# A sum of absolute differences: the kernel's instructions put into the first block, with semaphores of their own

**Chip, cores, metric.** One core of one Trainium2 chip. The metric is the device time of the kernel in microseconds (us). "The span" is what the profiler recorded of one execution; it is some 1.8 us shorter than the time.

## The reference

```python
batch, dim = 1024, 4096          # x, y: float32 [1024, 4096]
def reference(x, y, axis):       # axis = -1
    return np.sum(np.abs(x - y), axis=axis).astype(np.float32)
```

33.55 MB have to be read from memory; 4 KB are written.

## The kernel before

128 partitions hold 8 rows each (K = 8, H = 4). Rows 0 to 3 of x and y are loaded by two large transfers, rows 4 to 6 of x by a third; the y rows 4 to 6 go, one by one, into the y buffers that the first subtractions set free. The last row comes in four pieces. VectorE subtracts, ScalarE takes the absolute value and sums along the row. A semaphore is a counter that a finished transfer or operation raises and on which an instruction can wait (VectorE's first recorded wait starts 0.03 us after the landing at 41.49 us that it waits for). A block is a stretch of the built program that ends in a branch: the first block holds the opening barrier, the final one each engine's drain instructions and the closing barriers, in which GpSimd waits until all engines have drained (its wait is recorded at 83.89 us, 0.03 us behind the last of these drains, SyncE's at 83.86). A recording layer puts in the semaphores and waits (`tc`); only the first two loads and the first two waits of VectorE were placed by hand into the first block (`at_entry`).

```python
PIECES = [1984, 1088, 640, 384]; ROW6 = [2048, 1024, 1024]
at_entry(nc, lambda: nc.sync.dma_start(out=xa, in_=xr[:, 0:H, :]).then_inc(early[0], 16), "Drain")
at_entry(nc, lambda: nc.scalar.dma_start(out=yb, in_=yr[:, 0:H, :]).then_inc(early[1], 16), "Drain")
nc.sync.dma_start(out=xb[:, 0:H - 1, :], in_=xr[:, H:K - 1, :])
...
for sem in early:
    at_entry(nc, lambda: nc.vector.wait_ge(sem, 16), "UnconditionalBranch")
for k in range(H):
    whole(xa[:, k, :], yb[:, k, :], k)                    # tensor_sub, then activation with accum_out
    if k < H - 1:
        nc.sync.dma_start(out=yb[:, k, :], in_=yr[:, H + k, :])
        continue
    for w in PIECES: ...                                  # x piece and y piece, in turn
...                                                       # rows 4, 5; row 6 in three parts
for i, w in enumerate(PIECES):
    if i == 1:
        nc.vector.reduce_sum(out=ro[:, K - 2:K - 1], in_=part6, axis=AX)
    if i < n_part:
        nc.vector.tensor_sub(...); nc.scalar.activation(..., accum_out=last[:, i:i + 1])
    else:
        nc.vector.tensor_sub(out=last[:, n_part:n_part + w], ...)
        nc.vector.reduce_sum(out=ro[:, K - 1:K], in_=last, axis=AX, apply_absolute_value=True)
nc.sync.dma_start(out=orr, in_=ro)
```

Of the kernel before, what the change touches and what calls it, by code (L numbers as in the profile page):

```python
# [5 lines left out]

F32 = mybir.dt.float32
ABS = mybir.ActivationFunctionType.Abs
AX = mybir.AxisListType.X

PIECES = [1984, 1088, 640, 384]
ROW6 = [2048, 1024, 1024]


def at_entry(nc, emit, before):

    hook = nc.inst_callbacks[-1]
    lower = nc._always_lower_symbolic_ap
    nc.remove_inst_callback(hook)
    nc._always_lower_symbolic_ap = False  # L20
    try:
        ins = emit().ins
    finally:
        nc._always_lower_symbolic_ap = lower
        nc.push_inst_callback(hook)
    here = nc.cur_bb.bb.instructions
    main = nc.main_func.blocks[0].instructions
    at = [i for i, x in enumerate(here) if x.name == ins.name]
    assert len(at) == 1
    mine = here.pop(at[0])  # L30
    first = next(i for i, x in enumerate(main) if x.engine == mine.engine and x.opcode == before)
    main.insert(first, mine)


@with_exitstack
def kernel(ctx, tc, x, y, axis, out):
    nc = tc.nc
    P = nc.NUM_PARTITIONS
    R, C = x.shape
    K = R // P  # L40
    xr = x.rearrange("(p k) c -> p k c", p=P, k=K)
    yr = y.rearrange("(p k) c -> p k c", p=P, k=K)
    orr = out.rearrange("(p k) -> p k", p=P, k=K)
    assert sum(PIECES) == C
    n_part = len(PIECES) - 1
    n6 = len(ROW6)
    H = K // 2
    ps = ctx.enter_context(tc.tile_pool(name="ps", bufs=1))
    with tc.manual_schedule():
        xa = nc.alloc_sbuf_tensor("xa_rows", [P, H, C], F32).ap()  # L50
        xb = ps.tile([P, H, C], F32, tag="xb")

        yb = nc.alloc_sbuf_tensor("yb_rows", [P, H, C], F32).ap()
        ro = ps.tile([P, K], F32, tag="ro")
        part6 = ps.tile([P, n6], F32, tag="part6")

        last = ps.tile([P, n_part + PIECES[-1]], F32, tag="last")
        early = [tc.alloc_semaphore("early_x"), tc.alloc_semaphore("early_y")]
        at_entry(nc, lambda: nc.sync.dma_start(out=xa, in_=xr[:, 0:H, :]).then_inc(early[0], 16), "Drain")
        at_entry(nc, lambda: nc.scalar.dma_start(out=yb, in_=yr[:, 0:H, :]).then_inc(early[1], 16), "Drain")  # L60
        nc.sync.dma_start(out=xb[:, 0:H - 1, :], in_=xr[:, H:K - 1, :])

        def whole(tx, ty, k):
            nc.vector.tensor_sub(out=tx, in0=tx, in1=ty)  # L64
            nc.scalar.activation(tx, tx, ABS, accum_out=ro[:, k:k + 1])  # L65

        for sem in early:
            at_entry(nc, lambda: nc.vector.wait_ge(sem, 16), "UnconditionalBranch")  # L68
        for k in range(H):
            whole(xa[:, k, :], yb[:, k, :], k)  # L70
            if k < H - 1:
                nc.sync.dma_start(out=yb[:, k, :], in_=yr[:, H + k, :])
                continue
            o = 0
            for w in PIECES:
                nc.sync.dma_start(out=xb[:, k, o:o + w], in_=xr[:, K - 1, o:o + w])
                nc.sync.dma_start(out=yb[:, k, o:o + w], in_=yr[:, K - 1, o:o + w])
                o += w
        for k in range(H - 2):
            whole(xb[:, k, :], yb[:, k, :], H + k)  # L80
        o = 0
        for i, w in enumerate(ROW6):
            tx, ty = xb[:, H - 2, o:o + w], yb[:, H - 2, o:o + w]
            nc.vector.tensor_sub(out=tx, in0=tx, in1=ty)  # L84
            nc.scalar.activation(tx, tx, ABS, accum_out=part6[:, i:i + 1])  # L85
            o += w
        tx, ty = xb[:, H - 1, :], yb[:, H - 1, :]
        o = 0
        for i, w in enumerate(PIECES):
            s = slice(o, o + w)  # L90
            if i == 1:
                nc.vector.reduce_sum(out=ro[:, K - 2:K - 1], in_=part6, axis=AX)  # L92
            if i < n_part:
                nc.vector.tensor_sub(out=tx[:, s], in0=tx[:, s], in1=ty[:, s])  # L94
                nc.scalar.activation(tx[:, s], tx[:, s], ABS, accum_out=last[:, i:i + 1])  # L95
            else:
                nc.vector.tensor_sub(out=last[:, n_part:n_part + w], in0=tx[:, s], in1=ty[:, s])  # L97
                nc.vector.reduce_sum(out=ro[:, K - 1:K], in_=last, axis=AX, apply_absolute_value=True)  # L98
            o += w
        nc.sync.dma_start(out=orr, in_=ro)  # L100


# [1 line left out]
_INS = ['x', 'y', 'axis']  # L104
_OUTS = [((1024,), 'float32')]

_NUMBERS = {'axis': -1}


# [26 lines left out]
```

## Time and profile before

| | before |
|---|---|
| median time | 86.28 us (86.19 to 86.42, 3 runs) |
| span of the profiled run | 84.5 us |
| rows 0 to 3 of x and y landed, VectorE starts | 41.49, 41.80 us |
| last load landed | 80.68 us |
| final reduction starts | 81.53 us |
| store issued, landed | 82.11, 83.53 us |

How to read it: the loads run without a break to 80.7 us (DMA share 0.99 to 1.01 in every stage up to 78 us), and what follows the last landing is a tail of fixed steps. A gain must come from that tail, or from VectorE or ScalarE where the tail waits for them. The lines of the chain and of the last microseconds stand in the prediction. This is the view of the end line L131, one row per engine and operation: count, shortest, median and longest duration in ns, first and last start in us. SP is SyncE; q marks its sequencer.

```profile
L131 SPq EVENT_SEMAPHORE  x6: 17/28/28, 83.5 to 84.5; - x6
L131 SPq DRAIN  x3: 7/7/7, 83.8 to 84.1; - x3
L131 DVEq COMPARE_BRANCH  x1: 47/47/47, 41.6 to 41.6; - x1
```

Four of the six SyncE waits (28 ns each) stand between the store's landing at 83.5 and the first drain at 83.8; the other two belong to the final barriers. The one recorded branch is VectorE's, which carries a wait.

### The profile page before, as it was taken

The page shows a single profiled execution, that of the slowest core. Times are in us where ns is not written, and L with a number is a line of the kernel's source. Part 1 is how long each engine was busy: PE and PEld are TensorE (multiplying, and loading weights), DVE is VectorE, ACT ScalarE, POOL GpSimd, SP SyncE. Part 2 cuts the span into 40 slices and gives each one's busy share as a digit, 9 for nine tenths or more (in the row PEclk, how much of TensorE's full clock was granted, in tenths as well). Part 3 has the DMA queues.
Part 4 walks back from the last instruction along what each step waited for, and adds up shares of the span by engine and source line. Part 5 has one row for each costly group of instructions (what it writes and reads, how often), then busy time and mean ns, then how long its engine had stood idle before and what let it go on. Part 6 is the DMA issues. An engine that isn't in the chain of part 4 may idle for free.

```text
span 84.5 us, 110 instructions
## 1 busy us (share of the span) xinstructions
DVE 36.5 (43%) x15; ACT 31.2 (37%) x25; POOL 0.2 (0%) x4
## 2 busy tenths in 40 slices
DVE  0000000000000000000299999999298997988860
ACT  5000000000000000000001979797971968999950
POOL 0000000000000000000000000000000000000000
DMA  9479999995799999957999888999999999999700
GB/s 496 186 310 496 496 496 496 496 465 217 310 496 496 496 496 496 465 217 310 512 581 395 372 372 372 411 450 411 457 403 450 419 394 421 421 407 402 290 0 2
DMA packets 2160, 33.56 MB, mean 397 GB/s; under 512 B 368, under 2 KB 624, under 8 KB 1392
## 3 DMA queue, kind: packets, MB, share of 16 engines
q1 hardware_dynamic: 2016, 25.17, 70.8%
q10 hardware_dynamic: 144, 8.39, 22.9%
HBM read 33.55 MB, written 0.00 MB: 397 GB/s over the span
## 4 chain that ended last, share of the span: by engine, by line
DMA 67%; DVE 16%; ACT 13%; issue 1%; ACTq 0%; DVEq 0%
DMA yb_rows<-in_y_dram 67%; DVE xa_rows L64 10%; DVE xb L64 5%; ACT xb L85 5%; ACT xb L65 4%; ACT xb L95 4%; DVE ro L98 1%; ACTq L131 0%; DVEq L131 0%; DVEq L68 0%
## 5 line engine op out<-in xcount | busy, mean ns | idle before, releaser
L64 DVE TENSOR_TENSOR xa_rows<-xa_rows,yb_rows 128x4096 f32<-128x4096 f32 x4 | 17.4, 4420 | 41.8 <-DMA yb_rows<-in_y_dram 41.8
L65 ACT ACTIVATE xa_rows<-xa_rows 128x4096 f32<-128x4096 f32 x4 | 14.5, 3617 | 45.9 <-DVE xa_rows L64 45.9
L64 DVE TENSOR_TENSOR xb<-xb,yb_rows 128x4096 f32<-128x4096 f32 x2 | 8.9, 4426 | 2.0 <-DMA yb_rows<-in_y_dram 2.0
L65 ACT ACTIVATE xb<-xb 128x4096 f32<-128x4096 f32 x2 | 7.2, 3617 | 3.4 <-DVE xb L64 3.4
L84 DVE TENSOR_TENSOR xb<-xb,yb_rows 128x1024 f32<-128x1024 f32 (+1 forms) x3 | 4.6, 1576 | 0.5 <-DMA yb_rows<-in_y_dram 0.5
L94 DVE TENSOR_TENSOR xb<-xb,yb_rows 128x1984 f32<-128x1984 f32 (+2 forms) x3 | 4.3, 1447 | 0.9 <-DMA yb_rows<-in_y_dram 0.9
L85 ACT ACTIVATE xb<-xb 128x1024 f32<-128x1024 f32 (+1 forms) x3 | 4.0, 1323 | 0.0
L95 ACT ACTIVATE xb<-xb 128x1984 f32<-128x1984 f32 (+2 forms) x3 | 3.7, 1229 | 0.0
L65 ACT ACT_TABLE_LOAD x1 | 1.3, 1283 | 0.9 <-PEq L117 0.9
L65 ACT ACTIVATION_READ_ACCUMULATOR xa_rows<-xa_rows 128x1 f32 x4 | 0.7, 186 | 0.0
L98 DVE TENSOR_REDUCE ro<-last 128x1 f32<-128x387 f32 x1 | 0.6, 556 | 0.2 <-ACT xb L95 0.2
L97 DVE TENSOR_TENSOR last<-xb,yb_rows 128x384 f32<-128x384 f32 x1 | 0.6, 558 | 0.1
L95 ACT ACTIVATION_READ_ACCUMULATOR xb<-xb 128x1 f32 x3 | 0.6, 187 | 0.0
L85 ACT ACTIVATION_READ_ACCUMULATOR xb<-xb 128x1 f32 x3 | 0.6, 185 | 0.0
L65 ACT ACTIVATION_READ_ACCUMULATOR xb<-xb 128x1 f32 x2 | 0.4, 186 | 0.0
L92 DVE TENSOR_REDUCE ro<-part 128x1 f32<-128x3 f32 x1 | 0.2, 156 | 0.2 <-ACT xb L85 0.2
L117 POOL MEMSET const-bfloat16-1.0<- 128x1 bf16 x1 | 0.1, 101 | 0.0
L117 POOL MEMSET const-uint8-127<- 128x1 uint8 x1 | 0.1, 101 | 0.0
L117 POOL MEMSET const-float32-0.0<- 128x1 f32 x1 | 0.1, 98 | 0.2 <-issue 0.2
L117 POOL MEMSET const-float32-1.0<- 128x1 f32 x1 | 0.1, 98 | 0.0
## 6 DMA issues: line engine op xcount, KB each, us to landing
xb<-in_x_dram SPq DMA_DIRECT2D x1, 6144.0 KB, 54.9
yb_rows<-in_y_dram SPq DMA_DIRECT2D x3, 2048.0 KB, 15.0
xb<-in_x_dram SPq DMA_DIRECT2D x1, 992.0 KB, 17.6
yb_rows<-in_y_dram SPq DMA_DIRECT2D x1, 992.0 KB, 16.1
xb<-in_x_dram SPq DMA_DIRECT2D x1, 544.0 KB, 17.1
yb_rows<-in_y_dram SPq DMA_DIRECT2D x1, 544.0 KB, 17.9
xb<-in_x_dram SPq DMA_DIRECT2D x1, 320.0 KB, 18.3
yb_rows<-in_y_dram SPq DMA_DIRECT2D x1, 320.0 KB, 18.6
```

Of the source, the lines that this page charges most:

```text
L64: nc.vector.tensor_sub(out=tx, in0=tx, in1=ty)
L65: nc.scalar.activation(tx, tx, ABS, accum_out=ro[:, k:k + 1])
L84: nc.vector.tensor_sub(out=tx, in0=tx, in1=ty)
L85: nc.scalar.activation(tx, tx, ABS, accum_out=part6[:, i:i + 1])
L92: nc.vector.reduce_sum(out=ro[:, K - 2:K - 1], in_=part6, axis=AX)
L94: nc.vector.tensor_sub(out=tx[:, s], in0=tx[:, s], in1=ty[:, s])
L95: nc.scalar.activation(tx[:, s], tx[:, s], ABS, accum_out=last[:, i:i + 1])
L97: nc.vector.tensor_sub(out=last[:, n_part:n_part + w], in0=tx[:, s], in1=ty[:, s])
L98: nc.vector.reduce_sum(out=ro[:, K - 1:K], in_=last, axis=AX, apply_absolute_value=True)
L117: nc = _bacc.Bacc("TRN2", target_bir_lowering=False, num_devices=1)
```

## The change

The intent: put all of the kernel's instructions into the first block and give them their own semaphores, so that each piece needs one wait (x and y count on the same semaphore up to 32), no load waits for a reused semaphore, and one wait stands behind the store instead of one per semaphore. Transfers, operations, sizes and their order are the same.

```diff
-        for sem in early:
-            at_entry(nc, lambda: nc.vector.wait_ge(sem, 16), "UnconditionalBranch")
+    put(lambda: nc.sync.dma_start(out=xa, in_=xr[:, 0:H, :]).then_inc(s_first, 16), early=True)
+    put(lambda: nc.scalar.dma_start(out=yb, in_=yr[:, 0:H, :]).then_inc(s_first, 16), early=True)
+    put(lambda: nc.sync.dma_start(out=xb[:, 0:H - 1, :], in_=xr[:, H:K - 1, :]).then_inc(s_xb, 16))
...
+        put(lambda: nc.sync.dma_start(out=xb[:, H - 1, c], in_=xr[:, K - 1, c]).then_inc(s_piece[i], 16))
+        if i == 0:
+            put(lambda: nc.sync.wait_ge(s_sub, H))
+        put(lambda: nc.sync.dma_start(out=yb[:, H - 1, c], in_=yr[:, K - 1, c]).then_inc(s_piece[i], 16))
...
+        sub(xa[:, k, :], yb[:, k, :], [(s_first, 32)] if k == 0 else [])
...
+            sub(tx, ty, [(s_piece[i], 32)])
+            absum(tx, last[:, i:i + 1], s_end)
...
+    put(lambda: nc.sync.wait_ge(s_end, n_part + 3))
+    put(lambda: nc.sync.dma_start(out=orr, in_=ro).then_inc(s_out, 16))
+    put(lambda: nc.sync.wait_ge(s_out, 16))
```

(`put` moves what was just emitted in front of its engine's branch in the first block.)

## The prediction

> **What bounds the kernel now.** I read the page first (parts 1 and 2), then the chain that ended last in order of time, then the list of waits, and last the timeline of the final microseconds with the records of single lines.
>
> The page says that no engine is the bound:
>
> ```profile
> DVE 36.5 (43%) x15; ACT 31.2 (37%) x25; POOL 0.2 (0%) x4
> ...
> DMA  9479999995799999957999888999999999999700
> ...
> HBM read 33.55 MB, written 0.00 MB: 397 GB/s over the span
> ```
>
> The DMA row is full nearly to the end, and the bytes are fixed: two inputs of 16.78 MB. The stage table puts the DMA share at 0.99 from 0 to 70.5 us and at 1.01 from 70.5 to 78 us, with 420, 427, 423 and 410 GB/s. So the loads set where the work ends; what is not load is the start and the tail. The chain shows the same in order of time:
>
> ```profile
> 0.13 41.36 DMA yb_rows<-in_y_dram
> 41.49 0.03 issue
> 41.51 0.02 DVEq L68
> 41.53 0.05 issue
> 41.59 0.05 DVEq L131
> 41.63 0.16 issue
> 41.80 8.77 DVE xa_rows L64 x2
> ...
> 50.59 15.02 DMA yb_rows<-in_y_dram
> 65.61 0.02 issue
> 65.63 4.44 DVE xb L64
> 70.07 0.02 issue
> 70.09 3.71 ACT xb L65 x2
> 73.80 3.97 ACT xb L85 x6
> 77.77 3.63 ACT xb L95 x5
> 81.40 0.10 ACTq L131
> 81.50 0.02 issue
> 81.53 0.56 DVE ro L98
> ```
>
> Two things are to be seen. At 41.5 us VectorE has its data, but starts only at 41.80[...]. And from 70.09 to 81.50 us ScalarE works without a gap: the same stage by the stage table is 11.41 us long with 11.40 us of ScalarE busy. It is entered when the second yb row has landed (65.61) and its subtraction is done (4.44).
>
> The timeline of the end shows that a second path ends beside it:
>
> ```profile
> 79.81 0.82 DVE L94 TENSOR_TENSOR xb<-xb,yb_rows 128x640 f32<-128x640 f32 x1 [0.37 <-DMA yb_rows<-in_y_dram]
> 80.54 0.19 ACT L95 ACTIVATION_READ_ACCUMULATOR xb<-xb 128x1 f32 x1
> 80.66 0.74 ACT L95 ACTIVATE xb<-xb 128x640 f32<-128x640 f32 x1
> 80.77 0.56 DVE L97 TENSOR_TENSOR last<-xb,yb_rows 128x384 f32<-128x384 f32 x1
> 81.31 0.19 ACT L95 ACTIVATION_READ_ACCUMULATOR xb<-xb 128x1 f32 x1
> 81.53 0.56 DVE L98 TENSOR_REDUCE ro<-last 128x1 f32<-128x387 f32 x1 [0.19 <-ACT xb L95]
> 82.11 0.35 SPq L100 DMA_DIRECT2D out_dram<-ro  x1
> ```
>
> The 640-column y piece lands at 79.71 (issue at 61.08 plus 18.6), its subtraction runs 79.81 to 80.63, and its activation starts at 80.66, only 0.12 us after the accumulator read in front of it began. Where two accumulator read and activation pairs stand without a wait that distance is 0.09 us (75.51 to 75.60, 76.55 to 76.64, 79.45 to 79.54). So this activation is late by 0.03 us only: the tail is balanced between ScalarE and the landings.
>
> After the store's issue at 82.11 and its 1.4 us to landing, the records of the end line (L131) put four waits of SyncE at 83.54, 83.61, 83.67 and 83.74, its drain at 83.81 and the common barriers until 84.5.
>
> [...] L64, L94 and L97 have VectorE wait instructions of 21 ns. [...] the second xb subtraction, whose single wait it carries itself, starts 0.02 us after its landing (65.61 to 65.63), while the 384-column one, behind a wait instruction, starts at 80.77 after a landing at 80.68. [...] The trace has 47 ns for L131's, but 0.16 us more before the next instruction starts[...]. [...]
>
> **The change, part by part.** I compared the order and waits of the two built programs. Per engine the same operations stand in the same order with the same sizes. The separate wait calls of the source are folded into the instruction that follows, so the change does not add one wait instruction per wait; it takes them away. What differs:
>
> 1. First subtraction. Before: wait instruction, then a wait on the branch, then the operation at 41.80. After: the operation carries the one wait (count 32), so it should start about 0.02 us after the landing, near 41.52. That is 0.28 us earlier for VectorE. On the path: nothing. The fourth subtraction ends at 59.23 and the next waits 1.57 us for the first yb row, which lands at 60.71. That row is queued at 46.25 behind the 6.3 MB xb load, which lands near 55.8; queueing it at 45.97 does not move its place. 0.28 is less than 1.57: worth 0.
>
> 2. Piece loads. Before, the 384-column loads wait for reused semaphores of earlier rows, and are issued at 65.62 and 70.52. After, every load has its own semaphore pair and is issued by about 62.0 (six issues of some 0.44 us after 59.3). But their median time to landing was 14.6 and 10.2 us and the queue was full in between: 4 and 8 us earlier into a full queue. Worth 0.
>
> 3. One wait per piece. Four pieces and the fifth row lose a 21 ns wait instruction; the subtraction starts about 0.02 instead of 0.09 us after the landing: 0.07 us each. Row 5 had no such instruction, so ScalarE's 11.41 us stage is entered at the same time. The 1984 and 1088 pieces have their activations waiting behind ScalarE anyway. For the 640 piece 0.07 is on offer, but ScalarE is free only 0.03 earlier. For the 384 piece the subtraction would end near 81.26 instead of 81.33, and the final reduction waits for ScalarE at 81.50. So the sum at the final reduction is 0.03 us, not 5 x 0.07 = 0.35.
>
> 4. Final reduction and store. The reduction waits on one counter (5) instead of two; it started 0.02 after ScalarE's end and does so still. The store carries one wait. Worth 0.
>
> 5. End. Before: four wait instructions on SyncE, 0.065 us apart, so 0.26 us from the first one to the drain at 83.81. After: the wait for the store is folded into SyncE's branch to the final block, because nothing else follows it there. That is the form L68 and L131 had on VectorE: from the branch at 41.59 to the next instruction at 41.80 is 0.21 us, where a plain wait instruction took 0.065 to its successor. If SyncE pays the same 0.21, the gain is 0.26 - 0.21 = 0.05 us. If its branch costs as little as one wait, it is 0.26 - 0.065 = 0.20.
>
> 6. Instructions moved to the first block. The hop between blocks after the opening barrier goes away, but SyncE's xb issue at 0.92 goes into a queue filled for 41 us, and ScalarE's table load at 0.91 has until 46.26. Worth 0.
>
> Sum: 0.03 + 0.05 = 0.08 us, up to 0.23 us. I take 0.10: 86.28 - 0.10 = 86.18 us, a gain of 0.1%.
>
> **The rivals.** (a) All gains add up: 0.28 at the start, 0.35 at the pieces and 0.20 at the end give 0.83 us, 85.45 us, still only 1.0%. For it speaks only that each is real on its own engine; against it the 1.57 us of idle before the fifth subtraction, the full DMA row and ScalarE's gapless 11.41 us. (b) A wait takes the removed one's place: the branch on SyncE that now waits for the store is on the path where the old one was passed during the store's 1.4 us. [...] Nothing in the profile shows a larger branch cost. (c) The earlier queueing of the last pieces changes how the 16 DMA engines pace one another, so that the last landing at 80.68 moves. The landings of one piece spread over about 0.55 us across engines, so this could give or take 0.1 to 0.2 us: 86.0 to 86.4. Against it: no engine runs dry before or after. (d) The branch is cheap for SyncE: 86.05.
>
> **Range and chances.** The three times of before lie 0.23 us apart (86.19 to 86.42), more than my whole gain. Around 86.18 I allow rivals (b), (c) and (d) and that noise: 85.95 to 86.42. A gain over 2% needs 1.7 us; even rival (a) has half of that. A loss over 2% would need a load to be delayed by 1.7 us, and no load is issued later than before. So 0.01 faster, 0.98 same, 0.01 slower.
>
> **What would show it right or wrong.** In the new profile the first subtraction should start at about 41.5 with no separate wait in front, and the idle before the fifth should grow from 1.57 to about 1.8 us (step 1: the gain turned into waiting). The 384-column loads should be issued by about 62 us with times to landing near 18 to 19 us, and the last landing stay near 80.7 (step 2). VectorE should show no wait instructions at the pieces, their operations starting 0.02 us after landing, and ScalarE should stay gapless from 70.1 to about 81.47 (step 3). SyncE should show one branch of about 47 ns and some 0.2 us between the store's landing and its drain (step 5). The prediction is wrong if the last landing moves by over 0.3 us, or if ScalarE's gapless stage is entered earlier than 70.0, which would mean that the second yb row came in earlier and was not held by the queue.

From the landing at 41.49 to VectorE's start at 41.80 the chain shows L68's wait (21 ns), the branch of L131 (VectorE's, 47 ns) and 0.24 us of issue around them, 0.16 of it behind the branch, but not what happens in the issue time. 0.03 us at the pieces and 0.05 at the end make 0.08, up to 0.23 if SyncE's branch is cheap. Rival (b) lost the sentence with its 86.40 us, which was the author's estimate: it put SyncE's branch 0.2 us above VectorE's measured 0.21, so that the end would lose 0.15. No run shows such a branch. That the DMA engines pace one another, in rival (c) and in theory B of loads_late, is a conjecture put to the test; no run shows it.

## The result

| | before | after |
|---|---|---|
| median time | 86.25 us (86.19 to 86.53, 6 runs) | 86.10 us (85.90 to 86.27, 6 runs) |
| ratio | | 0.9977, 95% interval 0.9957 to 0.9998 |
| span of the profiled run | 84.5 us | 84.3 us |

A ratio here is the mean time of one kernel's fast runs over that of the other's in the same rounds, so it is not quite the ratio of the medians. By the 2% rule the two are the same; the 0.2% are small and only just clear of noise.

The chain that ended last, of the changed kernel (start us, us, what):

```profile
0.12 41.30 DMA yb_rows<-in_y_dram
41.43 0.02 issue
41.45 8.77 DVE xa_rows L105 x2
...
65.58 4.44 DVE xb_rows L105
70.02 0.02 issue
70.04 10.61 ACT xb_rows L110 x12
...
```

The wait, the branch and the 0.16 us of issue ahead of the first subtraction are gone: it starts 0.02 us after its data. ScalarE's last stage is entered at 70.04 instead of 70.09, about as much earlier as the first landing (41.43 instead of 41.49), ahead of which the change alters nothing in order or size. VectorE's timeline shows where the early start went (the idle time stands in brackets):

```profile
60.76 4.42 DVE L105 TENSOR_TENSOR xb_rows<-xb_rows,yb_rows 128x4096 f32<-128x4096 f32 x1 [1.88 <-DMA yb_rows<-in_y_dram]
65.58 4.43 DVE L105 TENSOR_TENSOR xb_rows<-xb_rows,yb_rows 128x4096 f32<-128x4096 f32 x1 [0.39 <-DMA yb_rows<-in_y_dram]
```

The idle before the fifth subtraction grew from 1.57 to 1.88 us. The last microseconds of both engines in the timeline, to be read against the same lines in the prediction:

```profile
79.68 0.83 DVE L105 TENSOR_TENSOR xb_rows<-xb_rows,yb_rows 128x640 f32<-128x640 f32 x1 [0.36 <-DMA yb_rows<-in_y_dram]
80.47 0.19 ACT L110 ACTIVATION_READ_ACCUMULATOR xb_rows<-xb_rows 128x1 f32 x1
80.56 0.72 ACT L110 ACTIVATE xb_rows<-xb_rows 128x640 f32<-128x640 f32 x1
80.66 0.56 DVE L138 TENSOR_TENSOR last_piece<-xb_rows,yb_rows 128x384 f32<-128x384 f32 x1 [0.15 <-DMA yb_rows<-in_y_dram]
81.19 0.19 ACT L110 ACTIVATION_READ_ACCUMULATOR xb_rows<-xb_rows 128x1 f32 x1
81.41 0.56 DVE L140 TENSOR_REDUCE ro_sums<-last_piece 128x1 f32<-128x387 f32 x1 [0.19 <-ACT xb_rows L110]
```

The 640-column activation now starts 0.09 us after the accumulator read in front of it (0.12 before), and it takes 0.72 instead of 0.74 us. SyncE's end, in the view of the end line:

```profile
L176 SPq DRAIN  x3: 7/7/7, 83.6 to 83.9; - x3
L176 SPq EVENT_SEMAPHORE  x2: 17/17/17, 83.8 to 84.3; - x2
L176 SPq COMPARE_BRANCH  x1: 32/32/32, 83.4 to 83.4; - x1
```

The four waits became one recorded branch of 32 ns. Read to the nanosecond, the branch starts at 83.413 and the drain at 83.564: 0.151 us, where the four waits took 0.263 (83.542 to 83.805).

To compare runs without the scatter of their landings I use three distances from here on. The **tail** runs from the start of the second xb row's subtraction (65.58 above) to the start of the final reduction (81.41). The **end** runs from SyncE's first instruction behind the store to its first drain. Where the wait for the store is put on that drain itself, the end is 0.000 by definition and shows nothing; there the third distance counts: **store to barrier**, from the store's issue on SyncE to GpSimd's gathering wait of the closing barrier.

| profile | tail, us | end, us | store to barrier, us | ratio to before (95%) |
|---|---|---|---|---|
| before | 15.893 | 0.263 | 1.784 | |
| before_again | 15.904 | 0.262 | 1.779 | |
| after | 15.826 | 0.151 | 1.672 | 0.9977 (0.9957 to 0.9998) |
| after_again | 15.823 | 0.155 | 1.680 | 0.9979 (0.9961 to 0.9997) |
| end_four | 15.821 | 0.268 | 1.783 | 0.9991 (0.9978 to 1.0004) |
| end_drain | 15.824 | 0.000 (by definition) | 1.524 | 0.9964 (0.9949 to 0.9979) |
| end_drain_again | 15.833 | 0.000 (by definition) | 1.518 | 0.9963 (0.9948 to 0.9979) |
| end_pool | 15.829 | – | 1.520 | 0.9967 (0.9947 to 0.9987) |
| loads_late | 15.876 | 0.151 | 1.678 | 0.9975 (0.9962 to 0.9988) |
| start_20 | 15.822 | 0.155 | 1.680 | 0.9979 (0.9960 to 0.9999) |
| start_60 | 15.814 | 0.152 | 1.685 | 1.0372 (1.0349 to 1.0395) |
| piece_2 | 15.879 | 0.155 | 1.682 | 0.9988 (0.9967 to 1.0009) |
| piece_4 | 16.173 | 0.152 | 1.670 | 1.0020 (1.0003 to 1.0036) |
| all_back | 15.892 | 0.268 | 1.782 | 1.0001 (0.9984 to 1.0018) |

The change took 0.07 us off the tail and 0.11 us off the end. Not quite all of these 0.18 us is left at the close. From SyncE's first drain to its second it was 0.065 us instead of 0.055. And GpSimd's clearing of the semaphores behind the barrier (the record EVENT_SEMAPHORE_RANGE_CLEAR) took 113 ns instead of 98, as it did in every kernel with semaphores of its own. Why is not shown. From the second xb row's subtraction to the end of the span it was 18.910 and 18.916 us in the two profiles of the kernel before, 18.749 and 18.755 in the two of the changed kernel. That is 0.16 us, and 0.16 / 86.25 is 0.2%.

### The profile page after: what moved, and what is told of

Read it like the earlier page. It is cut to its first block, busy times and chain, and to the rows that moved or that the text cites. A ratio compares the mean times of both kernels' runs of the same rounds, so it can differ in the third digit from the quotient of the medians.

```text
span 84.3 us, 98 instructions
## 1 busy us (share of the span) xinstructions
DVE 36.5 (43%) x15; ACT 31.2 (37%) x25; POOL 0.2 (0%) x4
## 4 chain that ended last, share of the span: by engine, by line
DMA 67%; DVE 16%; ACT 13%; ACTq 1%; issue 0%
DMA yb_rows<-in_y_dram 67%; ACT xb_rows L110 13%; DVE xa_rows L105 10%; DVE xb_rows L105 5%; ACTq L176 1%; DVE ro_sums L140 1%
## 5 line engine op out<-in xcount | busy, mean ns | idle before, releaser
L105 DVE TENSOR_TENSOR xb_rows<-xb_rows,yb_rows 128x4096 f32<-128x4096 f32 (+5 forms) x8 | 17.8, 2241 | 3.5 <-DMA yb_rows<-in_y_dram 3.4
L110 ACT ACTIVATE xb_rows<-xb_rows 128x4096 f32<-128x4096 f32 (+5 forms) x8 | 14.9, 1859 | 3.7 <-DVE xb_rows L105 3.7
L110 ACT ACTIVATION_READ_ACCUMULATOR xb_rows<-xb_rows 128x1 f32 x8 | 1.5, 188 | 0.0
L140 DVE TENSOR_REDUCE ro_sums<-last_piece 128x1 f32<-128x387 f32 x1 | 0.6, 556 | 0.2 <-ACT xb_rows L110 0.2
L138 DVE TENSOR_TENSOR last_piece<-xb_rows,yb_rows 128x384 f32<-128x384 f32 x1 | 0.6, 557 | 0.2 <-DMA yb_rows<-in_y_dram 0.2
```

Source lines behind the costliest of these rows:

```text
L105: put(lambda: nc.vector.tensor_sub(out=tx, in0=tx, in1=ty).then_inc(s_sub, 1))
L110: put(lambda: nc.scalar.activation(tx, tx, ABS, accum_out=to).then_inc(sem, 1))
L138: put(lambda: nc.vector.tensor_sub(out=last[:, n_part:n_part + w], in0=tx, in1=ty).then_inc(s_end, 1))
L140: put(lambda: nc.vector.reduce_sum(out=ro[:, K - 1:K], in_=last, axis=AX, apply_absolute_value=True).then_inc(s_end, 1))
```

## The experiments

My theory (A): the gain is these two terms, the tail and the end; the early start and the early loads are worth nothing. The rivals: the loads land earlier because of the change; every removed wait counts; the first block itself matters. Each kernel below is the changed kernel with one edit, unless said otherwise. All results were correct.

### The end

**end_four**: the end of the kernel before put back. A helper moves what is emitted after the kernel in front of the engine's first drain in the final block; nine waits become four wait instructions with two conditions each, and one on the drain.

```diff
-    put(lambda: nc.sync.wait_ge(s_out, 16))
+    return s_out, s_xb
 ...
+    in_final_block(nc, [lambda: nc.sync.wait_ge(s_out, 16)] * 9)
```

> The changed kernel with the end of the kernel before put back: four wait instructions and the drain's own wait in SyncE's final block, in place of the wait on the branch. Theory A (about half of the gain lies behind the store's landing: landing to SyncE's first drain 0.17 us in the changed kernel, 0.28 before): landing to drain returns to about 0.28, and the time is some 0.11 us above the changed kernel's, near 86.2, so a ratio to the kernel before near 0.999. Theory B (the gain came from loads that landed 0.06 us earlier because of the change, the end being worth nothing): ratio stays at 0.998. The step is as large as the scatter, so the trace's distance from landing to drain decides, the time only supports.

Measured: 86.18 us, 0.9991; the end went back to 0.268 us while the tail stayed at 15.821. So these 0.12 us of the end are due to the form of the wait. The time went the way that theory A has it, but its interval overlaps the changed kernel's: the trace shows it, the time only agrees.

**end_drain**: the same with a single wait, which lands on the drain; the branch has no wait and is passed while the store is in flight.

```diff
+    in_final_block(nc, [lambda: nc.sync.wait_ge(s_out, 16)])
```

> The changed kernel with the store's wait on SyncE's first drain in the final block, so that the branch is passed while the store is in flight. Theory A: the 0.15 us from the branch's start to the drain vanish: drain within 0.03 us of the landing, time 0.15 below the changed kernel's, near 85.95, ratio to the kernel before near 0.996. Theory B (the branch costs nothing by itself, the final barrier waits for something else): barrier and time stay, ratio 0.998.

Measured: 85.98 us, 0.9964, and beside the changed kernel again:

> The changed kernel again, beside the next two on one chip. Theory A: ratio to the kernel before again near 0.998 (0.9977 the first time); second yb row's subtraction to final reduction 15.82 us (15.826 the first time, 15.89 and 15.90 in the two profiles of the kernel before); landing to SyncE's first drain 0.17 us. Rival (the 0.2% are scatter): ratio within 0.001 of 1, these distances as in the kernel before.

> The changed kernel with the store's wait on SyncE's drain again. Theory A: 0.15 us (0.17%) below the changed kernel in the same call; ratio to the kernel before near 0.9962. Rival (its first result of 0.9964 owed something to early landings; its first landing came at 41.30 us): ratio 0.998, as the changed kernel's.

85.95 us and 0.9963, against 86.06 us and 0.9979 for the changed kernel. These figures agree with theory A: the branch's 0.15 us are on the path when it carries the wait, and off it when it does not. The trace decides it: from store to barrier 1.524 and 1.518 us, where the changed kernel took 1.672 and 1.680. This version is faster than the kernel before by 0.37%, clear of noise though far below the 2% rule. Against the changed kernel it is 0.16% in the second call, where both ran side by side, and 0.13% between the ratios of the first calls; there the intervals overlap. Its SyncE rows at the end line of the second profile have no branch left:

```profile
L190 SPq DRAIN  x3: 7/7/7, 83.4 to 83.7; - x3
L190 SPq EVENT_SEMAPHORE  x2: 17/17/17, 83.6 to 84.1; - x2
```

**end_pool**: the wait on GpSimd's drain, as GpSimd gathers the final barrier.

```diff
+    in_final_block(nc, [lambda: nc.gpsimd.wait_ge(s_out, 16)])
```

> The changed kernel with the store's wait on GpSimd's drain in the final block in place of SyncE's branch; GpSimd gathers the final barrier, and SyncE drains while the store is in flight. Theory A (the hop from SyncE's drains to GpSimd's gathering wait, 0.09 us in the run with SyncE's drain, leaves the path, GpSimd's own drain of 0.04 to 0.08 us comes in): within 0.05 us of the run with SyncE's drain, rather faster, ratio near 0.996. Rival (GpSimd sees the store's semaphore later than SyncE): slower than that run by 0.1 us.

Measured: 85.93 us, 0.9967 (0.9947 to 0.9987): within 0.05 us of end_drain, as expected, but not measurably better. From the first instruction that saw the store's semaphore to GpSimd's gathering wait it was 0.085 us (83.377 to 83.462) against 0.093 us with SyncE's drain (83.405 to 83.498): GpSimd's own drain costs what SyncE's two had cost.

### The loads

**loads_late**: the last four loads wait as they did before.

```diff
+        if i == 2:
+            put(lambda: nc.sync.wait_ge(s_xb, 16))
+        if i == 3:
+            put(lambda: nc.sync.wait_ge(s_row[1], 16))
         put(lambda: nc.sync.dma_start(out=xb[:, H - 1, c], ...).then_inc(s_piece[i], 16))
         ...
+        if i == 2:
+            put(lambda: nc.sync.wait_ge(s_row[0], 16))
+        if i == 3:
+            put(lambda: nc.sync.wait_ge(s_row[2], 16))
```

> The changed kernel with the last four loads waiting as before (384-column loads issued at about 65.6 and 70.5 us in place of 61.2 and 61.7). Theory A (the queue is full anyway): last landing at 80.6 to 80.7 us, times to landing back to about 14.6 and 10.2 us, time within 0.1 us of the changed kernel. Theory B (earlier queueing lets the 16 DMA engines pace one another better and is the cause of the 0.06 us earlier landings): last landing later by 0.05 us or more, time up by as much. The changed kernel's last issue took 2.7 us on SyncE; here it should take 0.33.

Measured: 86.11 us, 0.9975: no difference from the changed kernel in time. SyncE's timeline of that run, and below it that of the changed kernel:

```profile
65.58 0.33 SPq L97 DMA_DIRECT2D xb_rows<-in_x_dram  x1
70.48 0.33 SPq L104 DMA_DIRECT2D yb_rows<-in_y_dram  x1
```

```profile
61.23 0.44 SPq L93 DMA_DIRECT2D xb_rows<-in_x_dram  x1
61.71 2.67 SPq L96 DMA_DIRECT2D yb_rows<-in_y_dram  x1
```

The last load was issued 8.8 us earlier in the changed kernel, and its issue alone then took 2.67 us. One thing does not fit: in this one profile the tail was 0.05 us longer, because the pieces landed about 0.05 us later relative to the second yb row, and the last landing, at 80.69 instead of 80.63, was as late as theory B had it (and still inside theory A's 80.6 to 80.7). I put it down to scatter, not to the late issue, which one profile cannot show: the three other profiles with late loads (before, before_again, all_back) do not show it. Their 640-column subtraction starts 14.17 to 14.18 us after the second xb row's; less the 0.07 us of their separate wait that is 14.10 to 14.11, as in the changed kernel (14.10), while loads_late has 14.16. Their last load lands 15.07 to 15.09 us after the second yb row, in both profiles of the changed kernel 15.07 to 15.08, in loads_late 15.12.

**before_again** is the kernel before, unedited, for a second profile.

> The kernel before once more, for a second profile. Theory A: the first landing (41.49 us before, 41.43 after, with nothing different ahead of it) moves between executions of one program by 0.05 us or more, so the earlier landings of the changed kernel are scatter. Theory B: it is again at 41.49 and the second yb row again at 65.61, within 0.01.

Measured: its first rows landed at 41.35 us instead of 41.49 (the first subtraction starts at 41.66 instead of 41.80), its second xb row's subtraction starts at 65.54 instead of 65.63. So landings move by 0.1 us from execution to execution, and by more at times: in piece_2, with nothing different ahead of it, that subtraction starts at 65.96. After_again had its first subtraction at 41.31, end_four at 41.53. The 0.06 us by which the changed kernel's first profile was early lie inside this scatter; nothing shows them to be the change's doing.

### The start

**start_20** and **start_60** hold VectorE's first subtraction back by 20 and 60 satisfied wait instructions (two conditions each).

```diff
-        sub(xa[:, k, :], yb[:, k, :], [(s_first, 32)] if k == 0 else [])
+        sub(xa[:, k, :], yb[:, k, :], [(s_first, 32)] * 41 if k == 0 else [])   # start_60: * 121
```

> The changed kernel with 20 satisfied wait instructions ahead of VectorE's first subtraction: it starts about 1.3 us later (20 x 0.065), near 42.8. Theory A (the start has slack: VectorE idles 1.97 us before the fifth and 0.48 before the sixth subtraction of the changed kernel): time unchanged within 0.1 us; idle before the fifth falls from 1.97 to about 0.65. Rival (what the start saves counts in full): 1.3 us slower, ratio to the kernel before 1.013.

> The same with 60 such waits: first subtraction about 3.9 us later. Theory A: slack of 1.97 + 0.48 = 2.45 us is used up, so the end moves by 3.9 - 2.45 = 1.45 us, time near 87.55, ratio to the kernel before 1.015; ScalarE's gapless stage is entered near 71.5. Rival (in full): 3.9 us, ratio 1.043. Rival (DMA hides any of it): 0.998.

The 1.97 and 0.48 us in these expectations are slack, not idle: subtractions that wait for nothing start 4.335 us apart (each lasts 4.42). In the changed kernel the fifth starts 1.97 us more than that after the fourth, and the sixth 0.48 us more than that after the fifth.

Measured: 86.13 us, 0.9979 for start_20 and 89.49 us, 1.0372 (1.0349 to 1.0395) for start_60. My sizes were off, because a wait instruction with two conditions takes 0.098 us and not 0.065: the first subtraction came 1.94 us late in start_20 (43.39) and 5.79 us late in start_60 (47.24). With the measured delays theory A holds closely: 1.94 is inside the first 1.97 us of slack and cost nothing; of 5.79 us, 2.45 should be hidden, which leaves 3.34, and the final reduction came 3.33 us later (84.74 instead of 81.41). Two lines of VectorE's timeline in start_20, to be read against the pair of the changed kernel above:

```profile
60.77 4.42 DVE L105 TENSOR_TENSOR xb_rows<-xb_rows,yb_rows 128x4096 f32<-128x4096 f32 x1
65.59 4.43 DVE L105 TENSOR_TENSOR xb_rows<-xb_rows,yb_rows 128x4096 f32<-128x4096 f32 x1 [0.40 <-DMA yb_rows<-in_y_dram]
```

The 1.88 us of idle are used up, and the two rows start when they did. Start_60 shows one thing more in its list of waits:

```profile
DVE ro_sums L140 <- ACT xb_rows L110: 1.1, 1, 1.1
```

There all pieces had landed well before their use (the last at about 81.4 us, used at 83.09), no VectorE wait on a load is left in the list, and yet the tail was 15.814 us, as in the changed kernel. So after the change the tail is one subtraction of VectorE and then ScalarE's gapless work and the step to the final reduction; faster waits at the pieces could give no more than the 0.01 us between these two tails.

### The pieces

**piece_2** puts one wait instruction of its own back in front of each piece's subtraction, **piece_4** four (two conditions each).

```diff
-            sub(tx, ty, [(s_piece[i], 32)])
+            sub(tx, ty, [(s_piece[i], 32)] * 2)      # piece_4: * 9; the same for the last piece
```

> The changed kernel with a wait instruction of its own back in front of each of the four pieces, as before. Theory A: each piece's subtraction starts 0.07 us later after its landing (0.09 instead of 0.02), but only about 0.03 us of the 640-column piece reach the final reduction: time near 86.13. Rival (each removed wait counts): 4 x 0.07 = 0.28, time 86.38. The trace decides: distance of the 640-column activation from the accumulator read before it 0.12 in place of 0.09 us.

> The same with four wait instructions per piece, so each subtraction starts 0.07 + 3 x 0.065 = 0.265 us later. Theory A (ScalarE's queue of work covers the first pieces; the delay of the 640-column piece alone reaches the end, less the 0.03 us by which ScalarE was busy): final reduction 0.23 us later, time near 86.33. Rival (all add): 4 x 0.265 = 1.06 us, time 87.2.

Measured: piece_2 86.14 us, 0.9988, tail 15.879 us: 0.05 us more than the changed kernel, not 0.28. Its timeline shows the gap back:

```profile
80.86 0.19 ACT L110 ACTIVATION_READ_ACCUMULATOR xb_rows<-xb_rows 128x1 f32 x1
80.98 0.74 ACT L110 ACTIVATE xb_rows<-xb_rows 128x640 f32<-128x640 f32 x1
```

Piece_4: 86.48 us, 1.0020, tail 16.173 us: 0.35 us more. I expected 0.23, from waits of 0.065 us, and from the 640-column piece. The size was off because these waits take 0.098 us, so that one piece's delay is about 0.39 (4 x 0.098). And it was another piece that brought it to the end, the 1984-column one, for whose subtraction ScalarE now sat idle (counted from the end of the accumulator read before it):

```profile
78.04 1.86 ACT L110 ACTIVATE xb_rows<-xb_rows 128x1984 f32<-128x1984 f32 x1 [0.21 <-DVE xb_rows L105]
```

Counted from the second xb row's subtraction, this activation starts 0.301 us later than in the changed kernel (12.346 instead of 12.045); its subtraction is 0.369 us later, so ScalarE's earlier work covers 0.07. The gap at the 640-column piece adds only 0.017 to that, the longer run of both activations 0.03. One piece's delay reaches the end, not four: the rival's sum is 1.06 even at the smaller size.

### Everything back

**all_back** combines piece_2, loads_late, end_four and two wait instructions at the start, but keeps the own semaphores and the first block.

> The changed kernel with every wait of the kernel before put back (two wait instructions at the start, one per piece, the last four loads waiting, four waits and a drain at the end), but still with its own semaphores and in the first block. Theory A (two terms make the gain: 0.06 us at the pieces, 0.11 us at the end): both return, second yb row's subtraction to final reduction 15.88 to 15.90 us, landing to SyncE's drain 0.28 us, ratio to the kernel before 1.000 within 0.0015. Rival (the place in the first block or the allocation of buffers has a share): ratio stays near 0.998.

Measured: 86.25 us, 1.0001; tail 15.892, end 0.268. Both terms return, and no gain is left for the first block or the buffers' places: from the second xb row's subtraction to the end of the span it is 18.927 us, 0.01 to 0.02 more than in the kernel before, about what GpSimd's clearing takes longer (113 instead of 98 ns).

## Why the prediction was right

The time (86.10 against 86.18 us, range 85.95 to 86.42): right. That alone says little: the range is about three times as wide as the gain, no gain at all (86.25) would have lain inside it as well, and 86.10 lies nearer to rival (d), 86.05, than to 86.18. What counts is the steps, as the traces show them:

1. First subtraction, worth 0: right. It starts at 41.45, and the idle behind it grew to 1.88 us (foretold: about 1.8). Start_20 and start_60 show it causally.
2. Loads, worth 0: right. Loads_late costs no time. The last issue began at 61.7 us, as foretold, but blocked SyncE until 64.4, which was not; SyncE had nothing else to do.
3. Pieces, 0.03 us: the path was right in the main, the size about half (0.07 before to after, 0.05 in piece_2). I counted only the gap of the 640-column activation (0.125 to 0.093). Two activations that had waited also ran shorter once they stood ready: the 640-column one 721 instead of 737 ns, the 1984-column one 1844 instead of 1857; and the latter, which I had called covered, had started 0.003 us late. The sum is 0.032 + 0.016 + 0.013 + 0.003 = 0.064 us. That the 1984-column piece is covered was wrong: in before_again its activation started 0.030 us late and the 640-column one 0.020, and in piece_4 it brought most of the delay. I had also counted a wait instruction less at the fifth row; it stayed, as that row still waits on two semaphores (record at 60.69 us), at no cost.
4. Final reduction and store, worth 0: right. In both kernels the reduction starts about 0.02 us behind ScalarE's end, and from the store's issue to the next SyncE instruction it is 1.42 to 1.43 us.
5. End, 0.05 us: the mechanism was right, the size half. I took VectorE's 0.21 us for a branch with a wait; SyncE's took 0.15. The gain is 0.263 - 0.151 = 0.11 us; why SyncE's branch is shorter is not shown. The "up to 0.20" of a cheap branch was not reached by the change, but was by end_drain: 0.26 us less than before from store to barrier. The longer steps behind the first drain, about 0.03 us against the change, were not foreseen.
6. First block, worth 0: right. SyncE's third load is issued at 0.915 us before and 0.914 after, and all_back is at 1.0001.

So two terms were too small by about half, and one small loss was missed. That the sum stayed inside the range is owed to the range's width.

The rivals: (a), all gains add, is excluded by start_20 and piece_2. (b), a dearer branch, is excluded by the end of 0.15 us. (c), other pacing of the loads, is seen only as scatter, which is as large in the kernel before. (d), a branch as cheap as one plain wait (0.065 us), is excluded by the same 0.15 us, and end_drain shows that they count, by taking the wait off the branch. The time alone could not have told (d) from the prediction.

## What to carry to other kernels

Removing waits pays only where the wait is the last thing to end: here the waits taken from the start, from the pieces and from the last loads gave 0.07 us together, all of it at the pieces, because the loads' landings and ScalarE's gapless work stood behind the rest. The dearest waits were the ones that nothing covers, behind the last store; there it mattered which instruction carries the wait, and the drain was better than the branch or four waits (from store to barrier 1.52, 1.68 and 1.78 us). Where two engines run side by side this closely, one profile is not enough to call a piece covered: the 1984-column activation was 0.003 us late in one execution of the kernel before and 0.030 in the next. When effects are smaller than the scatter of the runs, compare distances inside the trace between events that the change can move, and put each piece back alone.

## What else the traces showed

- A branch with a wait, which the trace names COMPARE_BRANCH, took 0.15 us on SyncE (after) and 0.21 us on VectorE (before) to the next instruction's start (records of 32 and 47 ns). SyncE's opening branch without a wait cost nothing visible: its next load starts 0.083 us behind the barrier's wait with the branch between (before) and 0.082 without (after); and in end_pool its branch to the final block has 0.057 us at most, from the end of the store's issue to the drain.
- On VectorE a wait instruction with one condition took 0.066 us to the next start and one with two conditions 0.098 us; on SyncE two conditions took 0.06 to 0.07 us.
- The 640-column activation ran 736 to 737 ns where it started 0.033 to 0.034 us after the end of the subtraction that it needs, the shortest such distance seen, 730 and 727 at 0.040 and 0.044 (end_drain_again, end_pool), and 718 to 721 where that subtraction had ended 0.049 us or more before. The reason is not shown.
- SyncE's last load issue took 2.65 to 3.16 us in the runs where all loads were queued by 62 us, 0.72 and 0.49 us in start_20 and start_60, where it began at 63.7 and 67.5 us, and 0.33 us where it was held back to about 70.5.
